# One forward transform per block in the 31-tap convolution, the second product formed across partition halves

## The chip, the core and the metric

The kernel runs on one NeuronCore of one Trainium2 chip. The metric is the device time of one execution in microseconds (us); the time before is the median of three runs. TensorE does the matmuls and the transposes, VectorE (DVE in the profile) and ScalarE (ACT) read their results out of PSUM and work on SBUF, GpSimd (POOL) does side work, SyncE (SP) issues most of the DMAs.

## The reference, cut to what matters

The model has four layers; each has a token mixer and a convolutional gated MLP, for 256 context tokens and 256 latent tokens at width 1024. Layer 1 has the Conformer convolution as its mixer:

```python
def conformer_conv(h, w1, b1, wdw, bdw, lng, lnb, w2, b2):
    a = h @ w1 + b1
    u = a[..., :D_MODEL] * jax.nn.sigmoid(a[..., D_MODEL:])
    u = dwconv(u, wdw, bdw)
    u = jax.nn.silu(layernorm(u, lng, lnb))
    return u @ w2 + b2
```

`dwconv` is a depthwise convolution with 31 taps along the tokens, one filter for each of the 1024 channels. Only this step is touched.

## The kernel before, in words

All matmuls that need full accuracy are done as three (`mm3`, lines 153 to 158): both operands are split into a high and a low part, and high times high, high times low and low times high are accumulated. `split` (lines 166 to 168) makes the two parts: ScalarE writes the high part (line 167), then VectorE subtracts it (line 168). `load_w` (lines 132 to 148) does the same to each weight load of 1 MB: two VectorE subtractions of 128x1024 at line 145.

The convolution is done in the frequency domain, with blocks of at most 128 tokens. There are 2 token streams with 3 blocks each, and 4 groups of 256 channels: 24 block units. Each passes through three steps on TensorE, each followed by work on the other engines:

- `flip_in` (line 914): two transposes of the block to tokens-on-partitions, then `split`.
- `freq` (line 926): the forward transform. The 128 output partitions hold 64 cosine rows and 64 sine rows. The transform is run twice, with the rows in the order cosine, sine (matrix 0) and in the order sine, cosine (matrix 1), 3 matmuls of 256 columns each. VectorE multiplies the first result with the filter's table `KA[hc][0]` and the second with `KA[hc][1]` (line 936), adds the two products (line 937), and the sum is split (lines 167, 168).
- `back` (line 942): the inverse transform, 3 matmuls; a VectorE instruction (`stt`, line 164) adds the bias and sums the rows, ScalarE takes the squares (line 956).

`conv` (line 980) is a generator of one channel group: it yields after each step, and takes `back` of two steps ago, then `freq` of one step ago, then `flip_in`. `run()` (line 997) lets every active generator make one step; one such call is called a round below. A step has two blocks in most rounds. The rounds lie between units of 24 matmuls of the first projection (lines 1013 to 1030): for channel tiles 2 to 5 the unit has matmuls of 512 columns, for tiles 6 and 7 of 256 columns. After each pair of units, `glu` (line 1002) writes U[o] with a sigmoid on ScalarE and an `stt` on VectorE; the next `flip_in` reads U. After the last unit follow `layer_norm(0)` (line 959), two more rounds (lines 1036 and 1038) with matmuls of the conditioning in front of them (line 222, issued by `fill`), the transposes back (`turn`, line 1040, TensorE at line 1048, ScalarE at 1052), and the second projection.

TensorE's instructions are issued in the order of the program text (a manual schedule, line 1340). The order on the other engines is chosen by the framework's scheduler, not written by hand. Waits between engines are put in by the framework. PSUM tiles come from a pool of 7 banks, working tiles in SBUF from a pool of 35.

Of the kernel before, what the change touches and what calls it, by code (L numbers as in the profile page):

```python
# [16 lines left out]
ALU = mybir.AluOpType  # L17
AX = mybir.AxisListType

P = 128  # L20
# [59 lines left out]
def kernel(ctx: ExitStack, tc: tile.TileContext, xT, cT, cB, ada0, ada2, adaT1, adaT2, adaT3, prm, rows, rope, w_c, w_ug, w_o,  # L80
# [11 lines left out]
    def ps_mm():  # L92
        return pm.tile([P, T], F32, tag="mm", name="mm")
# [59 lines left out]
    def mm3(ps, a, b, start, stop):  # L153
        ah, al = a
        bh, bl = b
        nc.tensor.matmul(out=ps, lhsT=r(ah), rhs=r(bh), start=start, stop=False)  # L156
        nc.tensor.matmul(out=ps, lhsT=r(ah), rhs=r(bl), start=False, stop=False)  # L157
        nc.tensor.matmul(out=ps, lhsT=r(al), rhs=r(bh), start=False, stop=stop)  # L158

    def both(t, f):  # L160
        return f(t[0]), f(t[1])
# [4 lines left out]
    def split(hi, lo, src):  # L166
        nc.scalar.activation(out=r(hi), in_=src, func=AF.Copy)  # L167
        nc.vector.tensor_tensor(out=r(lo), in0=src, in1=hi, op=ALU.subtract)  # L168
# [722 lines left out]
    def conformer(li, nm):  # L891
        h = (HH, HL)
        b1 = col("cf_b1")
        raw = e_tile()
        nc.sync.dma_start(out=raw[:, 0:3 * P], in_=c_dft)
        dh, dl = g_tile(), g_tile()
        split(dh[:, 0:3 * P], dl[:, 0:3 * P], raw[:, 0:3 * P])
        brow = [e_tile(), e_tile()]
        KA = [[e_tile(), e_tile()] for _ in range(2)]
        for hc in range(2):  # L900
# [25 lines left out]
        def freq(g, s, b):  # L926
            c0, c1 = CGRP[g]
            w, hc, f0 = (c1 - c0) * P, c0 // 4, (c0 % 4) * P
            n = CBLK[b][1]
            v = VT.pop((g, s, b))  # L930
            t = []
            for i in range(2):
                ps = ps_mm()
                mm3(ps[:, 0:w], both((dh, dl), lambda a: a[0:n, i * P:(i + 1) * P]), v, True, True)
                t.append(e_tile()[:, 0:w])
                nc.vector.tensor_tensor(out=t[i], in0=ps[:, 0:w], in1=KA[hc][i][:, f0:f0 + w], op=ALU.mult)
            nc.vector.tensor_tensor(out=t[0], in0=t[0], in1=t[1], op=ALU.add)
            zh, zl = duo(w)
            split(zh[:, 0:w], zl[:, 0:w], t[0])
            Z[g, s, b] = (zh[:, 0:w], zl[:, 0:w])  # L940

        def back(g, s, b):
            c0, c1 = CGRP[g]
            w, hc, f0 = (c1 - c0) * P, c0 // 4, (c0 % 4) * P
            o0, n, p0 = CBLK[b][2:5]
            ps = ps_mm()
            mm3(ps[0:nb, 0:w], both((dh, dl), lambda a: a[:, 2 * P + p0:2 * P + p0 + nb]), Z.pop((g, s, b)), True, True)
            if f0 == 0:
                Y[hc, s, b] = e_tile()
            stt(Y[hc, s, b][0:n, f0:f0 + w], ps[0:n, 0:w], 1.0, brow[hc][0:n, f0:f0 + w], ALU.mult, ALU.add,  # L950
                accum_out=ysum[0:n, 3 * s + b, g:g + 1])
            i = 3 * s + b
            if g == 0:
                nc.gpsimd.tensor_scalar(out=shift[:, i:i + 1], in0=ysum[:, i, 0:1], scalar1=-1.0 / w, scalar2=None, op0=ALU.mult)
            junk = e_tile()
            nc.scalar.activation(out=junk[0:n, 0:w], in_=Y[hc, s, b][0:n, f0:f0 + w], func=AF.Square,
                                 bias=shift[0:n, i:i + 1], accum_out=vsum[0:n, i, g:g + 1])
# [423 lines left out]
def _tables():  # L1381
# [46 lines left out]
    g = np.concatenate([2.0 / m * c, 2.0 / m * s])  # L1428
    g[0] = 1.0 / m
    g[hf] = alt / m  # L1430
    c_dft = np.concatenate([np.concatenate([c, sn]).T, np.concatenate([sn, c]).T, g], 1).astype(f32)
    kk = np.arange(CONV_W) - CPAD
    tk = 2.0 * np.pi * (np.outer(kk, np.arange(hf)) % m) / m
    ca, sa = np.cos(tk), np.sin(tk)
    cn = ca.copy()
    cn[:, 0] = 1.0 - 2.0 * (kk % 2)
    c_k = np.concatenate([ca, cn, sa, -sa], 1).astype(f32)
    return rope, ztab, decay, dft, c_dft, c_k


# [84 lines left out]
```

## Time and profile before

| | us |
|---|---|
| median of the runs before | 2188.6 |
| lowest and highest of 3 runs | 2184.32 and 2189.11 |
| span of the profiled execution, first to last instruction | 2185.3 |

For the profiled execution the span is what is listed; the median of the runs lies 3.3 us above it and the lowest run 1.0 us below it. Rows of a timeline begin with the start in us and the duration in us of one instruction, or of several merged ones (x2: two in a row), then engine, line, operation, output and inputs, and in brackets the idle time of the engine in front of it with what released it.

### The profile page before, as it was taken

How to read it: one execution, taken by the hardware profiler on the slowest of the kernel's cores; microseconds unless marked ns; L12 is line 12 of the kernel's file. 1: busy time of each engine (PE TensorE's matmuls, PEld its weight loads, DVE VectorE, ACT ScalarE, POOL GpSimd, SP SyncE). 2: the span in 40 equal slices, each digit the busy share in tenths (PEclk: the TensorE clock that was granted, in tenths of full speed). 3: DMA queues.
4: the chain of work that ended last, by engine and by line, in shares of the span. 5: the costliest groups of instructions: out<-in, count | busy, mean ns of one | idle time of the engine just before them, and what ended most of it. 6: DMA issues, size and time to landing. Idle time of an engine off the chain costs nothing. (4 is left out here: it accounts for less than half of the span.)

```text
span 2185.3 us, 32167 instructions
## 1 busy us (share of the span) xinstructions
PE 2109.3 (97%) x12058; PEld 1801.1 (82%) x12058; DVE 1554.5 (71%) x2795; ACT 1286.7 (59%) x2774; POOL 257.7 (12%) x573
## 2 busy tenths in 40 slices
PE   5899999999999999999999999999999998898999
PEld 2767888888888979888888988898888887668999
DVE  4778368889756765668775677757979856976665
ACT  3688457677634465547654443456868754875553
POOL 2375210000020001000000200020000002620000
PEclk9999999999999999999999999999999999999999
DMA  8434134545432152444443222224555531114542
GB/s 316 171 115 159 67 122 174 212 174 197 170 129 83 54 195 86 152 152 170 177 169 103 95 78 78 97 78 157 193 192 193 209 110 48 59 42 157 188 177 94
DMA packets 49048, 305.36 MB, mean 140 GB/s; under 512 B 5597, under 2 KB 7133, under 8 KB 16252
## 3 DMA queue, kind: packets, MB, share of 16 engines
q1 hardware_dynamic: 47680, 301.17, 38.9%
q10 hardware_dynamic: 1212, 2.14, 0.3%
q8 instruction: 95, 1.56, 0.3%
q14 instruction: 61, 0.50, 0.1%
HBM read 299.09 MB, written 4.19 MB: 139 GB/s over the span
## 5 line engine op out<-in xcount | busy, mean ns | idle before, releaser
L156 PE MATMUL mm<-hh,whi 128*128 128x512 f32 (+1 forms) x1856 | 657.1, 354 | 0.0
L157 PE MATMUL mm<-hl,whi 128*128 128x512 f32 (+1 forms) x1856 | 654.4, 353 | 0.0
L158 PE MATMUL mm<-hh,wlo 128*128 128x512 f32 (+1 forms) x1856 | 654.3, 353 | 0.0
L145 DVE TENSOR_TENSOR wlo<-raw,whi 128x1024 fp32r<-128x1024 f32 (+2 forms) x362 | 430.9, 1192 | 289.8 <-PE mm L157 187.2
L142 ACT ACTIVATE whi<-raw 128x1024 fp32r<-128x1024 f32 (+3 forms) x370 | 374.9, 1019 | 238.0 <-PE mm L158 157.7
L156 PEld LDWEIGHTS mm<-hh,whi 128*128 128x128 f32 x1856 | 351.2, 189 | 51.6 <-issue 5.0
L158 PEld LDWEIGHTS mm<-hh,wlo 128*128 128x128 f32 x1856 | 351.0, 189 | 47.8
L157 PEld LDWEIGHTS mm<-hl,whi 128*128 128x128 f32 x1856 | 351.3, 189 | 46.3
L264 ACT ACTIVATE e<-e 128x512 f32<-128x512 f32 x512 | 315.9, 620 | 82.0 <-DVE e L263 82.0
L156 PE MATMUL mm<-g,whi 128*128 128x512 f32 (+1 forms) x936 | 318.7, 340 | 0.0
L157 PE MATMUL mm<-g,whi 128*128 128x512 f32 (+1 forms) x936 | 317.2, 339 | 0.0
L158 PE MATMUL mm<-g,wlo 128*128 128x512 f32 (+1 forms) x936 | 317.2, 339 | 0.0
L263 DVE TENSOR_TENSOR e<-raw,e 128x512 f32<-128x512 f32 x512 | 315.2, 683 | 0.0
L316 POOL TENSOR_TENSOR e<-e 128x256 f32<-128x256 f32 (+1 forms) x69 | 66.4, 962 | 1297.0 <-ACT e L314 1296.0
L157 PEld LDWEIGHTS mm<-g,whi 128*128 128x128 f32 x936 | 178.0, 190 | 19.6
L156 PEld LDWEIGHTS mm<-g,whi 128*128 128x128 f32 x936 | 178.0, 190 | 19.5
L158 PEld LDWEIGHTS mm<-g,wlo 128*128 128x128 f32 x936 | 178.1, 190 | 19.1
L167 ACT ACTIVATE g<-e 128x512 fp32r<-128x512 f32 (+1 forms) x137 | 76.3, 558 | 139.3 <-DVE e L512 48.3
L164 DVE SCALAR_TENSOR_TENSOR e<-mm,par,e 128x510 f32<-128x510 f32 (+3 forms) x186 | 126.1, 678 | 13.8 <-ACT e L506 9.8
L164 DVE SCALAR_TENSOR_TENSOR x<-mm,mod,x 128x256 f32<-128x256 f32 x192 | 85.3, 477 | 53.1 <-PE mm L158 52.9
L168 DVE TENSOR_TENSOR g<-e,g 128x512 fp32r<-128x512 f32 (+1 forms) x137 | 81.9, 598 | 55.7 <-ACT g L167 55.3
L506 ACT ACTIVATE e<-mm,par 128x512 f32<-128x512 f32 (+1 forms) x88 | 63.1, 717 | 63.5 <-PE mm L158 58.9
(260 smaller groups left out, 2850.2 us busy)
## 6 DMA issues: line engine op xcount, KB each, us to landing
raw<-in_w_fup_dram SPq DMA_DIRECT2D x88, 1024.0 KB, 4.8
raw<-in_adaT_dram SPq DMA_DIRECT2D x64, 1024.0 KB, 4.8
raw<-in_ada_dram SPq DMA_DIRECT2D x32, 1024.0 KB, 5.0
raw<-in_w_fd_dram SPq DMA_DIRECT2D x32, 1024.0 KB, 4.8
raw<-in_w_fd_dram SPq DMA_DIRECT2D x16, 768.0 KB, 5.1
raw<-in_w_p_dram SPq DMA_DIRECT2D x12, 1024.0 KB, 4.8
raw<-in_w_hi_dram SPq DMA_DIRECT2D x12, 1024.0 KB, 4.8
raw<-in_w_o_dram SPq DMA_DIRECT2D x8, 1024.0 KB, 4.8
```

The lines of the kernel that those rows point to most:

```text
L142: nc.scalar.activation(out=r(hi[:, 0:n]), in_=part, func=AF.Copy)
L145: nc.vector.tensor_tensor(out=r(lo[:, 0:n]), in0=part, in1=hi[:, 0:n], op=ALU.subtract)
L156: nc.tensor.matmul(out=ps, lhsT=r(ah), rhs=r(bh), start=start, stop=False)
L157: nc.tensor.matmul(out=ps, lhsT=r(ah), rhs=r(bl), start=False, stop=False)
L158: nc.tensor.matmul(out=ps, lhsT=r(al), rhs=r(bh), start=False, stop=stop)
L164: nc.vector.scalar_tensor_tensor(out=o, in0=a, scalar=s, in1=b, op0=op0, op1=op1, **kw)
L167: nc.scalar.activation(out=r(hi), in_=src, func=AF.Copy)
L168: nc.vector.tensor_tensor(out=r(lo), in0=src, in1=hi, op=ALU.subtract)
L263: nc.vector.tensor_tensor(out=t, in0=raw[:, q * D + (i % 2) * T:q * D + (i % 2 + 1) * T], in1=sb[i], op=ALU.mult)
L264: nc.scalar.activation(out=t, in_=t, func=AF.Copy, accum_out=asum[:, 2 * u + q, i // 2, i % 2:i % 2 + 1])
L316: nc.gpsimd.tensor_tensor(out=self.acc[:, a:b], in0=self.acc[:, a:b], in1=t[:, a:b], op=ALU.add)
L506: nc.scalar.activation(out=t[:, c0:T], in_=pg[:, c0:T], func=AF.Identity, bias=bd[:, li, j:j + 1], scale=wd[:, li, j, 1:2])
```

## The change

`freq` transforms each block once. One PSUM tile holds cosine rows in partitions 0 to 63 and sine rows in 64 to 127. Two VectorE instructions of 64 partitions each multiply one half with the table of the sine product and write the result into the other half of the output tile; a third multiplies the whole tile with `KA[hc][0]`. The table's second half has its sign order swapped to fit, matrix 1 is left out of the constant that is loaded, and `back` finds its matrix 128 columns earlier.

```diff
-        nc.sync.dma_start(out=raw[:, 0:3 * P], in_=c_dft)
+        nc.sync.dma_start(out=raw[:, 0:2 * P], in_=c_dft)
         dh, dl = g_tile(), g_tile()
-        split(dh[:, 0:3 * P], dl[:, 0:3 * P], raw[:, 0:3 * P])
+        split(dh[:, 0:2 * P], dl[:, 0:2 * P], raw[:, 0:2 * P])
...
-            t = []
-            for i in range(2):
-                ps = ps_mm()
-                mm3(ps[:, 0:w], both((dh, dl), lambda a: a[0:n, i * P:(i + 1) * P]), v, True, True)
-                t.append(e_tile()[:, 0:w])
-                nc.vector.tensor_tensor(out=t[i], in0=ps[:, 0:w], in1=KA[hc][i][:, f0:f0 + w], op=ALU.mult)
+            ps = ps_mm()
+            mm3(ps[:, 0:w], both((dh, dl), lambda a: a[0:n, 0:P]), v, True, True)
+            t = [e_tile()[:, 0:w], e_tile()[:, 0:w]]
+            hf = P // 2
+            for at, to in ((0, hf), (hf, 0)):
+                nc.vector.tensor_tensor(out=t[1][to:to + hf], in0=ps[at:at + hf, 0:w], in1=KA[hc][1][at:at + hf, f0:f0 + w], op=ALU.mult)
+            nc.vector.tensor_tensor(out=t[0], in0=ps[:, 0:w], in1=KA[hc][0][:, f0:f0 + w], op=ALU.mult)
             nc.vector.tensor_tensor(out=t[0], in0=t[0], in1=t[1], op=ALU.add)
...
-            mm3(ps[0:nb, 0:w], both((dh, dl), lambda a: a[:, 2 * P + p0:2 * P + p0 + nb]), Z.pop((g, s, b)), True, True)
+            mm3(ps[0:nb, 0:w], both((dh, dl), lambda a: a[:, P + p0:P + p0 + nb]), Z.pop((g, s, b)), True, True)
...
-    c_dft = np.concatenate([np.concatenate([c, sn]).T, np.concatenate([sn, c]).T, g], 1).astype(f32)
+    c_dft = np.concatenate([np.concatenate([c, sn]).T, g], 1).astype(f32)
...
-    c_k = np.concatenate([ca, cn, sa, -sa], 1).astype(f32)
+    c_k = np.concatenate([ca, cn, -sa, sa], 1).astype(f32)
```

## Rows read from the trace of the kernel before

**Rows 1.** The page: span's clock, and busy time, share and instructions of each engine

```profile
core 0: 2185.3 us, clock 0.990
...
PE 2109.3 (97%) x12058; PEld 1801.1 (82%) x12058; DVE 1554.5 (71%) x2795; ACT 1286.7 (59%) x2774; POOL 257.7 (12%) x573
```

**Rows 2.** Windows: length, busy PE, PEld, DVE, ACT, POOL, clock, DMA share, GB/s

```profile
684.00:731.00 47.00, 47.00 (x264) 40.90 (x263) 31.59 (x81) 20.61 (x48) 1.27 (x6) 1.00 0.19 68
731.00:770.00 39.00, 36.44 (x303) 35.52 (x305) 28.10 (x81) 17.46 (x51) 0.00 (x0) 1.00 0.16 55
770.00:787.00 17.00, 16.10 (x94) 7.83 (x87) 13.62 (x50) 11.24 (x25) 0.00 (x0) 0.80 0.52 189
787.00:1200.00 413.00, 411.87 (x2107) 347.02 (x2107) 278.08 (x440) 233.01 (x493) 15.88 (x35) 1.00 0.42 148
```

**Rows 3.** Timeline of PE: a round's first and last `freq` matmul, then `back`

```profile
744.35 0.28 PE L156 MATMUL mm<-g 75*128 75x256 f32 x1
...
745.66 0.28 PE L158 MATMUL mm<-g 113*128 113x256 f32 x1
...
749.55 0.28 PE L157 MATMUL mm<-g 128*98 128x256 f32 x1
```

**Rows 4.** Timeline of PE: its waits between 731 and 777 us

```profile
735.60 0.58 PE L920 MATMUL tr<-ident,e 128*113 128x128 f32 x3 [0.72 <-DVE e L164]
...
755.87 0.58 PE L920 MATMUL tr<-ident,e 128*113 128x128 f32 x3 [0.77 <-DVE e L164]
...
765.39 0.36 PE L157 MATMUL mm<-g 128*98 128x256 f32 x1 [1.06 <-DVE g L168]
...
776.60 4.33 PE L1048 MATMUL tr<-ident,e 60*128 60x60 f32 x22 [0.40 <-ACT e L975]
```

**Rows 5.** Line 936, both products of every block: count, min/median/max ns

```profile
L936 DVE TENSOR_TENSOR e<-mm,e x48: 402/414/426, 684.6 to 778.3; 128x256 f32<-128x256 f32 x48
```

**Rows 6.** Timeline of DVE: the chain of one round with two blocks

```profile
744.91 0.78 DVE L936 TENSOR_TENSOR e<-mm,e 128x256 f32<-128x256 f32 x2
745.72 0.42 DVE L937 TENSOR_TENSOR e<-e 128x256 f32<-128x256 f32 x1
746.06 0.74 DVE L936 TENSOR_TENSOR e<-mm,e 128x256 f32<-128x256 f32 x2
746.73 0.41 DVE L168 TENSOR_TENSOR g<-e,g 128x256 fp32r<-128x256 f32 x1
747.06 0.41 DVE L937 TENSOR_TENSOR e<-e 128x256 f32<-128x256 f32 x1
748.02 0.42 DVE L168 TENSOR_TENSOR g<-e,g 128x256 fp32r<-128x256 f32 x1 [0.54 <-ACT g L167]
```

**Rows 7.** Timeline of DVE, attention: the second reads partitions 64 up, writes 0 up

```profile
151.50 0.67 DVE L783 TENSOR_REDUCE mx<-mm 128x2 f32<-128x512 f32 x1
152.20 0.76 DVE L164 SCALAR_TENSOR_TENSOR g<-tr,gc,g 64x512 fp32r<-64x512 f32 x1
```

**Rows 8.** Timeline of DVE: a round's last split and `glu` before 735.60

```profile
733.76 0.43 DVE L168 TENSOR_TENSOR g<-e,g 128x256 fp32r<-128x256 f32 x1 [0.54 <-ACT g L167]
...
734.80 0.75 DVE L164 SCALAR_TENSOR_TENSOR e<-mm,par,e 128x512 f32<-128x512 f32 x1
```

**Rows 9.** Timeline of DVE: what stands ahead of PE's waits at 755.87 and 765.39

```profile
753.47 0.43 DVE L168 TENSOR_TENSOR g<-e,g 128x256 fp32r<-128x256 f32 x1 [0.54 <-ACT g L167]
754.19 1.23 DVE L145 TENSOR_TENSOR wlo<-raw,whi 128x1024 fp32r<-128x1024 f32 x1 [0.29 <-PE mm L157]
...
762.77 0.41 DVE L937 TENSOR_TENSOR e<-e 128x256 f32<-128x256 f32 x1
763.77 1.23 DVE L145 TENSOR_TENSOR wlo<-raw,whi 128x1024 fp32r<-128x1024 f32 x1 [0.59 <-PE mm L157]
764.91 0.42 DVE L168 TENSOR_TENSOR g<-e,g 128x256 fp32r<-128x256 f32 x1
```

**Rows 10.** Windows (columns as in rows 2): transposes and conditioning matmuls

```profile
780.00:786.00 6.00, 6.00 (x28) 1.45 (x27) 4.55 (x13) 4.74 (x12) 0.00 (x0) 0.50 0.33 109
```

## The prediction

> **What bounds the kernel now.** I read the page first: TensorE (PE) is busy for 97% of the span, with no other engine above 82% [rows 1]. Such a share says that PE time taken away is worth looking for, but not that all of it comes back, so the next view is the windows of the stage with the convolution [rows 2]. The reader should see three different stages there. From 684 to 731 us, between units with matmuls of 512 columns, PE is busy for 47.00 of 47 us: PE alone sets the pace, and VectorE has 15 us to spare. From 731 to 770 us, between units of 256 columns, PE is busy for 36.44 of 39 us and VectorE for 28.10: PE already waits for 2.6 us. From 770 to 787 us PE does transposes and conditioning matmuls at a mean clock of 0.80. Behind that, from 787 to 1200 us, PE idles for about 1 us in 413, so a gain in the stage reaches the end. The timeline says whom PE waits for in the second stage: each wait is released by VectorE [rows 4]. Two stand at the transposes of `flip_in`, which need U from `glu`, and one at the low part that `back` needs. The fourth, at 776.60, is for the normalization's ScalarE instructions.
>
> **What the change takes from PE.** Each block loses 3 matmuls of 256 columns. Twelve such matmuls of one round start from 744.35 to 745.66 [rows 3], so one takes 1.31/11 = 0.119 us from start to start (the 0.28 us of a row is its latency). A block saves 3 x 0.119 = 0.357 us, a round with two blocks 0.71 us, the 24 blocks 8.6 us, or 0.39% of the time. That is the ceiling.
>
> **What it adds to VectorE.** A block has three products instead of two; one of 128x256 takes 414 ns [rows 5]. The half-size ones stream as many columns, so I take the same duration for them. Two products in a row take 0.74 us together, so the second starts 0.33 us after the first [rows 6]: they overlap. The trace has no product that moves between partition halves. The nearest row is the attention instruction that reads PSUM partitions 64 and up and writes partitions 0 and up: it starts at 152.20, 0.03 us after its predecessor's end at 151.50 + 0.67 = 152.17 [rows 7]. No overlap there. So the price of the third product has two ends:
> - low end: all three overlap, and a block's chain gets 0.34 us longer, a round's 0.68 us;
> - high end: each of the three starts 0.03 us behind the end of the one before, 0.44 us each. The three take 1.32 us where 0.81 pass now from the first product to the sum (744.91 to 745.72), so +0.51 us in the first block. In the second, the first product waits for the end of the sum (+0.11), and products up to the next split take 1.22 instead of 0.67 us (746.06 to 746.73), so +0.55. Together +1.17 us per round.
>
> I take the high end, because rows 7 are the nearest thing to the new instructions. The Trainium skill's page "VectorE: DVE Perf Modes", section "Two Vector instructions with no wait between them", has the same as a rule: an instruction whose inputs or output start in another quadrant of 32 partitions than those of the last instruction starts only when every earlier Vector instruction has finished. By that rule all three products are held, also the full-size one behind the two halves. It speaks against this change; without it the sum would be the low end, below.
>
> **Where the saving stays.** 12 of the 24 blocks belong to the first two channel groups, whose rounds lie in the first stage; 10 of them are followed by a full unit of 512 columns. There the chain has time: a unit of 24 such matmuls lies between it and `back`. These keep it all: 10 x 0.357 = 3.6 us.
>
> **Where the chain comes to the path.** In the second stage only 24 matmuls of 256 columns lie between `freq` and `back`. For the round shown, the first product starts at 744.91 and the second block's `back` needs its low part at 749.55 [rows 3]: 4.64 us, while the chain takes 748.44 - 744.91 = 3.53 us [rows 6]. After the change PE arrives 0.71 us sooner, 3.93 us on, and the chain takes 4.70 us (low end 4.21). PE waits for 0.77 (0.28) us that it did not wait for before. Saved 0.71, lost 0.77: the round gives nothing, -0.06 us (low end +0.43). Round by round (plus is gain):
> - The last round of the first stage: behind its chain stand, in VectorE's queue, `back`'s instruction and then `glu` (733.76, 734.80), and the transposes at 735.60 wait for that `glu` [rows 8, 4]. The end of the chain moves by 1.17 (0.68) us. From the split's end at 734.19 to `glu` at 734.80 lie 0.61 us, of which `back`'s instruction takes some 0.34 (as the spacing above); the other 0.27 swallow a part: -0.9 (-0.4).
> - Two rounds like the one shown: -0.1 (+0.9) together.
> - The round before the wait at 755.87: its chain ends at 753.90, then come a weight subtraction at 754.19, after 0.29 us of idle time, then `glu`, then the transposes [rows 9, 4]. The chain moves by 1.17 (0.68), less 0.29: -0.9 (-0.4). The idle row before it is all the cover there is.
> - The round before the wait at 765.39: two weight subtractions stand inside this chain, the second in front of the last split. The sum at 762.77 moves to about 763.9, the subtraction behind it from 763.77 to 764.3, and so does the split at 764.91 [rows 9]: -0.5 (0).
> - The next round has one block, so a chain of half the length before a unit of the same length: it keeps +0.36.
> - The last `freq` round, three blocks: PE would be done 1.07 us earlier, but the transposes behind it wait for the normalized rows, as at 776.60 [rows 4], and that chain isn't shortened: 0. The longer product chain, up to 1.7 us more, delays the high and low parts for the second projection; PE reaches that only behind the conditioning matmuls, which it runs at half clock [rows 10], and it takes the channel tiles one by one, so I count nothing for it. Without this cover it would cost up to 1.7 us.
>
> Edits counted as nothing: the constant's load and its split are a third smaller (the split goes in the queues of ScalarE and VectorE behind the norm of the first units, well before the first product at 684.6 [rows 5]; its gain is under one instruction of 0.42 us [rows 6]). One PSUM bank less is taken per block, but no wait in the stage is for a bank. The swapped table costs no instruction. No DMA is moved, and POOL isn't touched.
>
> **The sum.** 3.6 - 0.9 - 0.1 - 0.9 - 0.5 + 0.36 = 1.5 us gain at the high end; at the low end 3.6 - 0.4 + 0.9 - 0.4 + 0 + 0.36 = 4.0 us. The span of 2185.3 us [rows 1] would become 2183.8. The median of the runs lies 3.3 us above that span, and I keep the distance: 2188.6 - 1.5 = 2187.1 us. The runs before differ by 4.8 us among themselves, so about 0.2% (4.4 us) is what can be told from no change.
>
> **The rivals.**
> - Overlap after all: the half products run like the pairs at 744.91, the low end: 2188.6 - 4.0 = 2184.6 us. For it: pairs do overlap [rows 6]. Against it: rows 7.
> - All of PE's time comes back: 2188.6 - 8.6 = 2180.0 us. It needs an order on VectorE in which `glu` and the splits come ahead of what stands before them now; the order is the scheduler's, and may change. For it: VectorE's busy time after the change is about 28.1 + 9 x 0.5 = 32.6 us (nine blocks between 731 and 770) in a stage of some 36 us: it fits, just. Against it: the four waits [rows 4], three of which lie behind the very chain that gets longer.
> - Slower, by the clock. In the 6 us from 780 on PE runs at 0.50 of its clock, after some 3 us of transposes only [rows 10]. The change takes half the matmuls out of the last `freq` round, right before, and leaves waits in their place. If the lower level (1.2 GHz) began some 4 us sooner, with the transposes at 776.60, that stretch of 4.33 us [rows 4] could take up to twice as long: net 1.5 - 4.0, so 2188.6 + 2.5 = 2191.1 us. It decides from the point where the low level costs more than the 1.5 us gained: at half speed that is 3 us of PE's work sooner. For it: the row with the low clock follows a thin stretch. Against it: nine dense matmuls of that round are left, and the clock stood at full level through all waits of the second stage [rows 2].
> - The change does nothing that can be seen: VectorE takes back the 3.6 us of the first stage as well, 2188.6 us. Against it: 15 us of slack there [rows 2].
>
> **How the numbers follow.** Forecast 0.48; overlap 0.22; all of it 0.12; slower by the clock 0.10; nothing 0.08. The range leaves out most of the full gain below and little above: from 2181.0 to 2191.5 us. Faster by over 0.2% (under 2184.2) takes the full gain (0.12), half of the overlap case (0.11) and a little of the forecast (0.04): 0.27. Slower by over 0.2% (over 2193) takes the clock case with a bad draw and little else: 0.08. The rest is 0.65.
>
> **What would show it.** Right: 36 `freq` matmuls less in each half of the groups; three products per block of about 0.41 us that don't overlap; the first stage about 3.6 us shorter; more waits of PE for `glu` and for the low part between 731 and 770 us, 2 to 3 us more in all. Wrong: product pairs 0.34 us apart; no new waits, and a stage 8 us shorter; a low clock ahead of 779 us; or a different order on VectorE, with `glu` ahead of the products, which would move every one of these waits.

## The result: slower by 13 us, and the profile after

The changed kernel takes 2201.5 us (median of 4 runs, 2195.3 to 2206.4) against 2188.2 for the kernel before beside it (2184.3 to 2189.1). The ratio is 1.0064, with a 95% interval of 1.0044 to 1.0083. The forecast was 2187.1 us, and the upper end of the range was 2191.5.

The page after, first the span with its clock, then the line of the engines (compare [rows 1]):

```profile
core 0: 2201.3 us, clock 0.985
...
PE 2118.4 (96%) x11986; PEld 1800.8 (82%) x11986; DVE 1570.2 (71%) x2819; ACT 1286.6 (58%) x2774; POOL 257.3 (12%) x573
```

TensorE has the 72 matmuls less that were announced, and yet is busy for 9 us longer: it ran more of its work at the lower clock (mean 0.985, before 0.990). VectorE has 24 instructions more.

To see where the time went I cut the stage in three, by landmarks that every variant has: **A**, from the first transposes of `flip_in` to those of the seventh round that has any; **B**, from there to the first transposes of `turn`; **C**, from there to the last transposes of `turn`. Windows of the kernel before, in these three stretches (columns as in [rows 2]):

```profile
677.65:734.67 57.02, 57.02 (x326) 49.94 (x324) 36.92 (x92) 24.53 (x56) 1.27 (x6) 1.00 0.21 74
734.67:775.60 40.93, 37.93 (x309) 35.01 (x307) 30.45 (x99) 19.62 (x53) 0.00 (x0) 1.00 0.25 84
775.60:804.20 28.60, 28.14 (x186) 19.38 (x184) 17.86 (x61) 18.04 (x42) 1.47 (x2) 0.87 0.46 174
```

The same stretches of the changed kernel:

```profile
683.12:741.75 58.63, 54.69 (x289) 46.02 (x288) 45.39 (x106) 24.88 (x58) 2.19 (x6) 0.99 0.21 72
741.75:788.20 46.45, 38.85 (x273) 33.59 (x271) 35.13 (x105) 18.59 (x52) 0.00 (x0) 0.94 0.21 71
788.20:821.10 32.90, 30.91 (x185) 20.95 (x185) 21.16 (x66) 19.31 (x43) 1.45 (x2) 0.77 0.44 157
```

A is 1.6 us longer, B 5.5, C 4.3: 11.4 us in all. TensorE had no idle time in A and now has 3.9 us; in B its idle time goes from 3.0 to 7.6 us although it has fewer matmuls; and its mean clock falls from 1.00 to 0.94 in B and from 0.87 to 0.77 in C. Behind C little differs: 1381.1 us to the end before, 1380.2 after. The spans differ by more, 16.0 us, because the work ahead of the stage took 5.5 us longer in this execution (683.1 to 677.6). Of that work the kernels here change only the load and split of the constant, and its end lay anywhere from 676.9 to 684.0 us from one kernel's profile to the next. So the stage is compared from its own first transposes.

Where TensorE waits now: three waits in A, then its last and longest, then the two longest of B (timeline of PE; compare [rows 4]):

```profile
698.23 0.50 PE L156 MATMUL mm<-hh,whi 128*128 128x512 f32 x1 [0.52 <-DVE e L164]
712.29 0.36 PE L157 MATMUL mm<-g 128*98 128x256 f32 x1 [0.96 <-DVE g L168]
728.00 0.50 PE L156 MATMUL mm<-hh,whi 128*128 128x512 f32 x1 [0.50 <-DVE e L164]
...
740.76 0.52 PE L156 MATMUL mm<-g 128*98 128x256 f32 x1 [1.31 <-ACT g L167]
...
765.55 0.36 PE L156 MATMUL mm<-g 128*98 128x256 f32 x1 [1.89 <-ACT g L167]
...
776.84 0.36 PE L156 MATMUL mm<-g 128*98 128x256 f32 x1 [1.89 <-ACT g L167]
```

Before, TensorE waited for `glu` and once, for 1.06 us, for a low part (two waits in front of `freq`, at 772.80 and 773.46, took 0.17 and 0.28 us). Now it waits for the splits in front of `back` (L156 and L157 on a tile `g`): in two of A's rounds, and in nearly every round of B. The waits at 698.23 and 728.00 are at the first matmul of a unit, released by an eviction on VectorE; I read them as a PSUM bank that was not yet free. The prediction had found no wait for a bank in the kernel before, and priced none.

VectorE's chain of the first round (its timeline; L936 are the half products, L937 the full product, L938 the sum, L168 the split's subtraction; compare [rows 6]):

```profile
689.02 1.23 DVE L145 TENSOR_TENSOR wlo<-raw,whi 128x1024 fp32r<-128x1024 f32 x1 [3.55 <-PE mm L157]
690.26 0.86 DVE L936 TENSOR_TENSOR e<-mm,e 64x256 f32<-64x256 f32 x2
691.15 0.42 DVE L937 TENSOR_TENSOR e<-mm,e 128x256 f32<-128x256 f32 x1
691.61 0.43 DVE L938 TENSOR_TENSOR e<-e 128x256 f32<-128x256 f32 x1
692.06 0.86 DVE L936 TENSOR_TENSOR e<-mm,e 64x256 f32<-64x256 f32 x2
692.95 0.43 DVE L168 TENSOR_TENSOR g<-e,g 128x256 fp32r<-128x256 f32 x1
693.41 0.42 DVE L937 TENSOR_TENSOR e<-mm,e 128x256 f32<-128x256 f32 x1
693.87 0.42 DVE L938 TENSOR_TENSOR e<-e 128x256 f32<-128x256 f32 x1
694.84 0.42 DVE L168 TENSOR_TENSOR g<-e,g 128x256 fp32r<-128x256 f32 x1 [0.55 <-ACT g L167]
```

Nothing overlaps: each instruction starts 0.01 to 0.04 us behind the end of the one in front of it, the full product too; the last one waits for ScalarE's high part. The chain takes 694.84 + 0.42 - 690.26 = 5.00 us; the same round of the kernel before takes 3.50 us.

In two rounds of B a weight subtraction stands between the last product and the sum that needs it (same view):

```profile
774.44 0.42 DVE L937 TENSOR_TENSOR e<-mm,e 128x256 f32<-128x256 f32 x1
774.78 1.21 DVE L145 TENSOR_TENSOR wlo<-raw,whi 128x1024 fp32r<-128x1024 f32 x1
775.92 0.42 DVE L938 TENSOR_TENSOR e<-e 128x256 f32<-128x256 f32 x1
```

The sum starts 1.48 us behind the product, not 0.46 (691.15 to 691.61): 1.02 us in the chain, and TensorE's wait of 1.89 us at 776.84 follows.

The low clock in windows of its own (a stretch behind the wait of 1.31 us at 740.76, and one in `turn`; compare [rows 10]):

```profile
741.00:744.00 3.00, 3.00 (x13) 2.52 (x13) 1.85 (x6) 1.91 (x7) 0.00 (x0) 0.50 0.00 0
789.00:798.00 9.00, 8.72 (x35) 4.17 (x39) 7.57 (x20) 4.47 (x11) 0.00 (x0) 0.50 0.19 76
```

A granted clock of 0.50 is the lower level, 1.2 GHz. In C, the clock of 0.77 makes 2 x 0.23 x 32.9 = 15.1 us at half speed, against 2 x 0.13 x 28.6 = 7.4 before: half of the difference, 3.8 us, is lost. The same working gives B, at 0.94 for 1.00, a loss of 0.06 x 46.5 = 2.8 us, and A 0.6. So up to 7 of the 11.4 us are the lower clock, an estimate that counts each of these stretches as bound by TensorE.

### The profile page after: what moved, and what is told of

Same layout as the page of the kernel before. It is cut to its first block, busy times and chain, and to the rows that moved or that the text cites. A ratio compares the mean times of both kernels' runs of the same rounds, so it can differ in the third digit from the quotient of the medians.

```text
span 2201.3 us, 32050 instructions
## 1 busy us (share of the span) xinstructions
PE 2118.4 (96%) x11986; PEld 1800.8 (82%) x11986; DVE 1570.2 (71%) x2819; ACT 1286.6 (58%) x2774; POOL 257.3 (12%) x573
## 4 chain that ended last, share of the span: by engine, by line
PE 54%; ACT 2%; DVE 2%; POOL 1%; issue 1%; ACTq 0%; POOLq 0%; DVEq 0%
PE mm L156 16%; PE mm L157 16%; PE mm L158 16%; PE mm L442 2%; PE mm L448 1%; PE mm L832 1%; PE tr L811 0%; ACT hh L364 0%; PE mm L347 0%; DVE mx L777 0%; POOL rsy L201 0%; ACT g L794 0%; ACT g L814 0%; ACT whi L142 0%; ACT e L343 0%
## 5 line engine op out<-in xcount | busy, mean ns | idle before, releaser
L156 PE MATMUL mm<-hh,whi 128*128 128x512 f32 (+1 forms) x1856 | 658.4, 355 | 1.0 <-DVE e L164 1.0
L157 PE MATMUL mm<-hl,whi 128*128 128x512 f32 (+1 forms) x1856 | 655.7, 353 | 0.0
L145 DVE TENSOR_TENSOR wlo<-raw,whi 128x1024 fp32r<-128x1024 f32 (+2 forms) x362 | 430.5, 1192 | 290.3 <-PE mm L157 177.5
L156 PEld LDWEIGHTS mm<-hh,whi 128*128 128x128 f32 x1856 | 351.3, 189 | 52.7 <-issue 4.0
L157 PEld LDWEIGHTS mm<-hl,whi 128*128 128x128 f32 x1856 | 351.5, 189 | 46.6
L156 PE MATMUL mm<-g,whi 128*128 128x512 f32 (+1 forms) x936 | 318.2, 340 | 0.0
L157 PE MATMUL mm<-g,whi 128*128 128x512 f32 (+1 forms) x936 | 316.6, 338 | 0.0
L157 PEld LDWEIGHTS mm<-g,whi 128*128 128x128 f32 x936 | 176.8, 189 | 19.7
L156 PEld LDWEIGHTS mm<-g,whi 128*128 128x128 f32 x936 | 176.8, 189 | 19.5
L168 DVE TENSOR_TENSOR g<-e,g 128x512 fp32r<-128x512 f32 (+1 forms) x137 | 81.9, 598 | 56.6 <-ACT g L167 55.6
L164 DVE SCALAR_TENSOR_TENSOR x<-mm,mod,x 128x256 f32<-128x256 f32 x192 | 85.1, 476 | 50.8 <-PE mm L158 50.6
```

The source lines that it names most:

```text
L145: nc.vector.tensor_tensor(out=r(lo[:, 0:n]), in0=part, in1=hi[:, 0:n], op=ALU.subtract)
L164: nc.vector.scalar_tensor_tensor(out=o, in0=a, scalar=s, in1=b, op0=op0, op1=op1, **kw)
```

## The experiments

All with the stretches as above, from one profiled execution each, and the ratio to the kernel before run beside it. That kernel's median was 2188.0 us beside e1 to e4 and e13 to e16, but 2184.4 beside e5 to e8 and 2187.0 beside e9 to e12, so times of different sets are compared by their ratios. "Forward" is how often a block is transformed.

| kernel | forward | A | B | C | ratio and 95% interval |
|---|---|---|---|---|---|
| before | 2 | 57.0 | 40.9 | 28.6 | |
| the change | 1 | 58.6 | 46.5 | 32.9 | 1.0064 [1.0044, 1.0083] |
| e1, two products in place | 1 | 53.4 | 37.6 | 30.5 | 0.9968 [0.9956, 0.9979] |
| e2, third product in place | 1 | 55.8 | 42.7 | 32.9 | 1.0022 [1.0011, 1.0033] |
| e3, halves in the kernel before | 2 | 59.1 | 44.1 | 27.9 | 1.0048 [1.0031, 1.0065] |
| e4, ScalarE moves the halves | 1 | 63.5 | 57.6 | 30.7 | 1.013 [1.011, 1.015] |
| e5, change, forward transforms first | 1 | 59.6 | 53.5 | 31.2 | 1.009 [1.0072, 1.0109] |
| e6, before, forward transforms first | 2 | 57.4 | 42.7 | 28.1 | 1.0017 [1.0007, 1.0028] |
| e7, change, wide instructions | 1 | 54.3 | 41.4 | 30.7 | 1.002 [1.0008, 1.0032] |
| e8, e7 and e5 together | 1 | 56.2 | 50.8 | 31.1 | 1.0061 [1.0046, 1.0076] |
| e9, change, weights on GpSimd | 1 | 55.1 | 46.9 | 31.2 | 1.005 [1.0036, 1.0064] |
| e10, before, wide instructions | 2 | 57.0 | 40.9 | 29.8 | 1.0009 [0.9997, 1.0021] |
| e11, e7 and e9 together | 1 | 54.3 | 42.9 | 31.6 | 1.0014 [1.0004, 1.0024] |
| e12, before, weights on GpSimd | 2 | 56.7 | 41.1 | 26.8 | 1.0002 [0.999, 1.0015] |
| e13, wide change early, before late | mixed | 54.3 | 40.1 | 26.9 | 0.9978 [0.9969, 0.9988] |
| e14, change in late groups only | mixed | 57.1 | 48.2 | 30.0 | 1.0025 [1.0014, 1.0035] |
| e15, e9 and the next weights too | 1 | 54.7 | 47.5 | 31.8 | 1.0046 [1.0034, 1.0058] |
| e16, change in early groups only | mixed | 57.9 | 42.1 | 28.2 | 1.0014 [1.0005, 1.0023] |

### What the third product and the halves cost

e1 forms the second product as one full instruction in place, so that a block has two products again (the move between the halves is left out):

```diff
-            for at, to in ((0, hf), (hf, 0)):
-                nc.vector.tensor_tensor(out=t[1][to:to + hf], in0=ps[at:at + hf, 0:w], in1=KA[hc][1][at:at + hf, f0:f0 + w], op=ALU.mult)
+            nc.vector.tensor_tensor(out=t[1], in0=ps[:, 0:w], in1=KA[hc][1][:, f0:f0 + w], op=ALU.mult)
```

> One forward transform per block, but only two full-size products, both in place: the swap of the halves is left out, and with it the third VectorE instruction. PSUM tiles per round are as in the changed kernel (6, not 8). Theory (VectorE's longer chain is the whole loss): most of the 8.6 us of matmuls come back, 2179 to 2184 us, against 2188 before and 2201 after; the chain of a two-block round is 3.5 us as before, products of a block 0.33 to 0.37 us apart. Rival (PSUM tiles: with 6 per round instead of 8 a unit's bank waits for another reader): still slower than before, 2190 us or more, with PE waiting for back's instruction at the head of units.

e2 has three products again, all of 128 partitions and in place; the third goes to columns that nobody reads (the move between the halves is left out here too):

```diff
+            for o in (t[1], junk):
+                nc.vector.tensor_tensor(out=o, in0=ps[:, 0:w], in1=KA[hc][1][:, f0:f0 + w], op=ALU.mult)
```

> One forward transform, three full-size products that all read and write from partition 0 on: the table product is done twice, the second time into columns that nothing reads; the swap is left out. The same number of VectorE instructions as the changed kernel, none of them in another partition half. Theory (the loss comes from instructions in another half, each of which starts only behind the end of the one before): the three products overlap, 0.33 us apart, a round's chain is about 4.2 us, and the time is 2182 to 2190 us. Rival (only the count of instructions matters): as the changed kernel, 2197 us or more.

e3 keeps both transforms of the kernel before and cuts its second product in two half instructions that stay in their own partitions:

```diff
+                for q in ((slice(0, P),) if i == 0 else (slice(0, P // 2), slice(P // 2, P))):
+                    nc.vector.tensor_tensor(out=t[i][q], in0=ps[q, 0:w], in1=KA[hc][i][q, f0:f0 + w], op=ALU.mult)
```

> The kernel before with its two transforms; only the second product is done in two instructions of 64 partitions, each in its own half, so nothing moves between halves. PE has all its old work, VectorE three products. Theory (instructions that start in another half wait for the end of the one before): the lower half's product and the one behind it are held, a chain is 0.7 to 1.2 us longer, and since no matmul is saved the time is 2198 to 2212 us. Rival (only a write into the other half is dear): products 0.33 us apart, and 2189 to 2196 us.

e1 took 2181.4 us, e2 2192.0, e3 2197.3 beside 2188.0 for the kernel before. The windows of e1, stretches A and B:

```profile
677.89:731.25 53.36, 52.86 (x290) 45.52 (x288) 37.46 (x94) 25.19 (x58) 1.27 (x6) 1.00 0.23 79
731.25:768.90 37.65, 34.63 (x274) 30.92 (x272) 29.12 (x96) 18.56 (x51) 0.00 (x0) 1.00 0.25 87
```

So the transform's time does come back where VectorE's part stays as it was: A falls by 3.7 us, and TensorE is hardly idle there. e1 has the change's six PSUM tiles per round, so these aren't the loss. e2 and e3 fell outside what their theories gave (2182 to 2190 and 2198 to 2212 us). The chain of a round is 3.51 us in e1, 4.30 in e2, 5.00 in the change. A chain longer by 0.79 us costs 10.6 us of median, another 0.70 us costs 9.5; in the stage alone (A, B and C together) it is 9.9 and 6.6. These are two prices, the instruction itself and its hold (that it starts only at the end of the one in front), of the same order. e2 is also the prediction's low end, where the third product overlaps: 2184.6 us were given for it, 2192.0 came. e2's chain shows the overlap that the change lacks (timeline of DVE):

```profile
691.30 0.75 DVE L936 TENSOR_TENSOR e<-mm,e 128x256 f32<-128x256 f32 x2
691.96 0.42 DVE L168 TENSOR_TENSOR g<-e,g 128x256 fp32r<-128x256 f32 x1
692.29 0.42 DVE L937 TENSOR_TENSOR e<-mm,e 128x256 f32<-128x256 f32 x1
```

Here an instruction starts 0.33 us behind the start of its predecessor, in the change 0.43 to 0.46. This agrees with the rule of the Trainium skill, page "VectorE: DVE Perf Modes", section "Two Vector instructions with no wait between them", that an instruction whose inputs or output begin in another quadrant than the last one's waits for all earlier ones to finish. e3 shows that moving between halves isn't needed for it (timeline of DVE; L937 are the products, the x2 a full one and the half at partitions 0 to 63, the last the half at 64 to 127):

```profile
687.14 0.75 DVE L937 TENSOR_TENSOR e<-mm,e 128x256 f32<-128x256 f32 x2
687.82 0.41 DVE L168 TENSOR_TENSOR g<-e,g 128x256 fp32r<-128x256 f32 x1
688.26 0.43 DVE L937 TENSOR_TENSOR e<-mm,e 64x256 f32<-64x256 f32 x1
688.72 0.43 DVE L938 TENSOR_TENSOR e<-e 128x256 f32<-128x256 f32 x1
```

The half at partition 0 overlaps like a full product; the half at partition 64, which stays in its own partitions, waits for the end of the split in front of it, and starts 0.44 us behind it. One more instruction per block with such a hold costs the kernel before 9 us of median.

e4 has ScalarE copy the halves crosswise, and VectorE form two products:

```diff
-                nc.vector.tensor_tensor(out=t[1][to:to + hf], in0=ps[at:at + hf, 0:w], in1=KA[hc][1][at:at + hf, f0:f0 + w], op=ALU.mult)
+                nc.scalar.activation(out=sw[to:to + hf], in_=ps[at:at + hf, 0:w], func=AF.Copy)
+            nc.vector.tensor_tensor(out=t[1], in0=sw, in1=KA[hc][1][:, f0:f0 + w], op=ALU.mult)
```

> One forward transform; ScalarE copies the two halves of the result crosswise into SBUF (two instructions of 64x256 per block, some 0.37 to 0.42 us each, 48 in all), VectorE does the two full-size products of the kernel before. The result is the reference's. Theory: VectorE has its old load, ScalarE (busy for half of the stage) takes 18 us more beside; a chain gets about 0.5 us longer by the copies: 2180 to 2190 us, at or below before. Rival (any step more in the chain costs as much, on whichever engine): 2196 us or more.

2215.7 us, the slowest of all. The chain, now from ScalarE's first copy, takes 5.56 us, and the second block's copies stand behind the first block's split in ScalarE's queue. Taking work from VectorE doesn't help if the path from `freq` to `back` gets longer by it.

### Where the reader of the chain stands

e5 changes the order in a round, the same for e6 from the kernel before:

```diff
-                for f, at in ((back, i - 2), (freq, i - 1), (flip_in, i)):
+                for f, at in ((freq, i - 1), (back, i - 2), (flip_in, i)):
```

> The changed kernel, but in each round the two forward transforms are issued ahead of the two back transforms of the round before, instead of behind them. VectorE's chain (first product to last subtraction, 5.00 us for two blocks) stays as it is; what waits for it on TensorE comes later by the six matmuls of two forward transforms (0.21 us each, so 1.3 us). Theory (the lost time is TensorE waiting for the end of that chain, and the low clock behind these waits): TensorE's idle time in the stage falls from 13.5 to about 5 us, the stage from 138 to 122 to 127 us, total 2185 to 2191. Rival 1 (VectorE's time itself is what limits, wherever the reader stands): stage 135 us or more, total 2198 to 2203. Rival 2 (the forward transforms, now 1.3 us earlier behind the transposes, wait for the split of these instead): TensorE's waits move to VectorE's and ScalarE's split of the transposes, total above 2195.

> The same move of the forward transforms ahead of the back transforms in the kernel before. Theory: its chain of 3.50 us is nearly covered, TensorE is idle for only 3.45 us of the stage, so at most these can be had: 2184.5 to 2188.5. Rival 2 of the run above (the split of the transposes is late instead): above 2190, and the waits name that split. Against the run above it tells what the move does where there are no halves.

My theory failed here: 2204.8 us for e5 where it wanted 2185 to 2191, and 2190.3 for e6, with the kernel before at 2184.4. The waits of TensorE in e5's stage (us in total, times, longest):

```profile
PE mm L156 <- ACT g L167: 8.4, 5, 3.4
PE tr L920 <- DVE e L164: 3.8, 3, 1.3
PE mm L156 <- DVE e L937: 2.9, 2, 1.5
```

In the changed kernel the first stood at 6.8 us, all but 0.2 of it in front of `back`, and the other two weren't there. In e5 only 1.5 of its 8.4 us are in front of `back`; the rest is in front of `freq`. The transposes now wait for `glu`, the next unit's first matmul for a bank that a product has to free, and the forward transform for the split of the transposes, which stands behind the chain in the queues of VectorE and ScalarE: rival 2. A reader that comes later gains nothing where all others stand behind the same queue. So it isn't the chain's length alone that counts, but what is queued on VectorE in a round.

e7 makes the queue shorter: the two blocks of a round lie side by side in one PSUM tile, and the products, the sum and the split are done once on 512 columns. e8 has e5's order on top of it. e10 is the same widening for the kernel before. In the cut, `wide` and `spectrum` are views of the tile and of the table over both blocks:

```diff
+            for j, (s, b) in enumerate(todo):
+                mm3(ps[:, j * w:(j + 1) * w], both((dh, dl), lambda a: a[0:n, 0:P]), VT.pop((g, s, b)), True, True)
+            for at, to in ((0, hf), (hf, 0)):
+                nc.vector.tensor_tensor(out=wide(t[1])[to:to + hf], in0=wide(ps)[at:at + hf], in1=spectrum(1, at), op=ALU.mult)
+            nc.vector.tensor_tensor(out=wide(t[0]), in0=wide(ps), in1=spectrum(0, 0), op=ALU.mult)
```

> The changed kernel, with the two blocks of a round side by side in one PSUM tile, so that the two half products, the full product, the sum and the split each run once on 512 columns and not twice on 256: 5 VectorE instructions and one of ScalarE per round for 10 and 2. Estimate from the rows of 256 columns (0.42 us, of which some 0.15 us would be saved by each pair): chain of about 4.5 us, but it can begin only when both transforms are done, 0.6 us later, and the two blocks no longer overlap, ScalarE's part standing bare. Theory (length of the chain from the end of the transforms): about as the change or a little better, 2195 to 2202. Rival (the number of held VectorE instructions): with half as many, 2186 to 2192.

> Both edits: wide instructions, and the forward transforms ahead of the back transforms. Theory: 1.3 us of slack more per round covers most of what is left of the chain: 2181 to 2187, below both kernels. Rival 1 (VectorE's time itself): as the wide kernel without the move, 2 us either way. Rival 2 (late split of the transposes): above the wide kernel without the move.

> The kernel before with both transforms kept, and the two blocks of a round side by side in one PSUM tile per transform: two products, a sum and a split of 512 columns in place of twice as many of 256. Against the changed kernel in the same wide form (2188.8 in the runs before) it tells what the one transform itself brings where VectorE has room. Theory (full queue of VectorE): 8 instructions of a round become 4, some 0.6 us less; the kernel before has little idle time left (2.6 us in the first part), so 2182 to 2187. Rival (chain alone: the blocks no longer overlap and begin 0.7 us later): 2187 to 2193.

e7 takes 2188.8 us, 0.2% above the 2184.4 beside it: the number of held instructions (the rival) came true, the length of the chain alone didn't. Its chain of a round (timeline of DVE; L943 the half products, L944 the full one, L945 the sum):

```profile
685.78 1.39 DVE L943 TENSOR_TENSOR e<-mm,e 64x512 f32<-64x512 f32 x2
687.20 0.69 DVE L944 TENSOR_TENSOR e<-mm,e 128x512 f32<-128x512 f32 x1
687.93 0.69 DVE L945 TENSOR_TENSOR e<-e 128x512 f32<-128x512 f32 x1
689.38 0.69 DVE L168 TENSOR_TENSOR g<-e,g 128x512 fp32r<-128x512 f32 x1 [0.76 <-ACT g L167]
```

4.29 us in place of 5.00, with 5 instructions for 10. A falls to 54.3 us, nearly e1's 53.4; B, at 41.4, does no better than the kernel before. e8 loses as e5 did (2199.3 us, 2181 to 2187 expected). e10 (2187.8 us) is the kernel before within the uncertainty: TensorE had no idle time in A to win back.

### What else stands in VectorE's queue

In the changed kernel the weight subtraction (L145, 1.22 us) has no idle time in front of it in four of its eight places in A; before, it always had some, 1.37 us or more. A round there lasts 7.34 us on TensorE (e1), and VectorE has to do 5.0 us of chain, 1.22 of subtraction, 0.74 of split, 0.8 of two evictions and `glu`'s 0.75 in every second round. That is over 8 us in such a round, and the trace has the same: the chains of the change start at 690.26, 698.55 and 706.32 us, 8.29 and 7.77 us apart. e9 gives the subtraction of outputs 2 to 7 to GpSimd, e12 does so in the kernel before, e11 in e7:

```diff
+        lo_eng[0] = nc.gpsimd
         for o in range(2, 6):
             w = load(o)
...
-            nc.vector.tensor_tensor(out=r(lo[:, 0:n]), in0=part, in1=hi[:, 0:n], op=ALU.subtract)
+            (lo_eng[0] or nc.vector).tensor_tensor(out=r(lo[:, 0:n]), in0=part, in1=hi[:, 0:n], op=ALU.subtract)
```

> The changed kernel, with the subtraction of the weights' second parts (1.22 us on VectorE, one per round of the first ten rounds or so) given to GpSimd for the weights of outputs 2 to 7 of this stage. The chain itself stays: three products of 0.45 us per block. Theory (what counts is all that stands in VectorE's queue of a round: chain, split of the transposes, evictions and the weight subtraction, against a round of some 7.2 us on TensorE; the change filled it): VectorE has 12 subtractions of 1.22 us less, its queue fits again, TensorE's idle time in the first part of the stage falls from 10.7 to 3 to 5 us, the low clock there goes, total 2188 to 2193 against 2201. Rival (only the length of the chain between the forward and the back transform counts; the subtraction stands outside it in most rounds): not below 2197. Rival 2 (GpSimd takes about twice as long, about 2.5 us from 1.28 us for 512 columns, and the weights are late, or it slows VectorE's instructions beside it): VectorE's instructions lengthen, or TensorE waits for GpSimd; 2200 or more.

> The kernel before with the weight subtraction of this stage on GpSimd. Theory: its VectorE had room (63 of 94 us busy in the first part), TensorE is idle there for 2.6 us, so it gains at most these: 2183 to 2188. It is the control of the changed kernel with the same edit: if this one gains as much, the edit says nothing of the change.

> The changed kernel with wide instructions and with the weight subtraction on GpSimd. Theory (full queue): of the wide kernel's 6.8 us of idle TensorE in the first part 4 to 5 go, total 2182 to 2186, below both kernels. Rival (chain alone): 2187 to 2190, as the wide kernel.

e9 is at 2198.7 us, so in the total the rival came nearer. By stretches both were right, each in one place: A falls from 58.6 to 55.1 us, and its first five intervals from transposes to transposes are 6.63, 7.34, 13.48, 6.65 and 7.35 us, e1's within 0.01 (the change: 6.64, 7.34, 15.50, 6.95, 7.34). The sixth, the last of A, stays at 13.66, with 14.86 in the change and 11.90 in e1. B stays at 46.9. The control e12 gains 0.3 us in A and nothing in B. e11 (2190.5 us, 2182 to 2186 expected) adds nothing to e7, whose rounds already fitted.

### Early and late rounds apart

e16 makes the change for channel groups 0 and 1 only, whose rounds lie behind long units, e14 for groups 2 and 3 only (`g >= 2` in the same line); e15 is e9 with the end of its stretch moved behind the next projection's loads, and so puts the next projection's weight subtractions, those inside the chain, on GpSimd as well. The edit of e16:

```diff
-                for f, at in ((back, i - 2), (freq, i - 1), (flip_in, i)):
+                for f, at in ((back, i - 2), ((freq_once if g < 2 else freq), i - 1), (flip_in, i)):
```

> From the kernel before: only groups 0 and 1 as in the change (one transform, half products of 256 columns), groups 2 and 3 with two transforms. Theory (in the changed kernel the first six rounds lose only where a weight subtraction and the chain fill VectorE's round): first six rounds 57 to 58.6 us, the rest 36 us, total 0 to 2 us above before. With the run of the late groups it splits the change's 13 us.

> From the kernel before: only groups 2 and 3 as in the change. Theory: the first six rounds 57.0 us as before; from there to the last transposes about 41 us for 36 (chain of 5 us behind units of 2.8 us), and some 4 us more at the low clock after it; total 7 to 11 us above before. Rival (the loss is spread over all rounds alike): 4 to 6 us above before, and the groups 0 and 1 alone as much.

> The changed kernel with all weight subtractions of the stage on GpSimd, those of the next step's weights too, which stand between the last product and the sum in two of the short rounds. Theory (what stands inside the chain pays in full): the first six rounds 54 to 55 us (58.6; 55.1 with the first loads alone), the two rounds of 13.3 us fall to 11.5 to 12, the rest to 38 to 40 us (42.0), total 2190 to 2195. Rival (only the chain's own instructions count): the rest stays at 41 to 42 us, total 2197 or more.

e16 is 0.14% slower (2190.3 us), e14 0.25% (2193.5). Their stages are 1.6 and 8.7 us longer than that of the kernel before, 10.3 of the change's 11.4; the medians add up to less, 2.2 and 5.5 of 13 us, and the rest isn't assigned. e14's median lies in the range of its rival (4 to 6 us), but e16's isn't as much, as that rival would have it. By the stages, then, most of the loss is in the late rounds, where 24 matmuls of 0.12 us lie between `freq` and `back`. Part of it is the clock: e14's B has a mean of 0.89, which by the working above is 5.3 of its 48.2 us. The two long waits are there in e14 with the same length (timeline of PE):

```profile
757.06 0.36 PE L156 MATMUL mm<-g 128*98 128x256 f32 x1 [1.89 <-ACT g L167]
...
769.71 0.53 PE L156 MATMUL mm<-g 128*98 128x256 f32 x1 [1.89 <-ACT g L167]
```

e15 should have shortened them, and made them 2.46 us. The sum took the subtraction's place as the slow one. VectorE in that round:

```profile
757.10 0.42 DVE L939 TENSOR_TENSOR e<-mm,e 128x256 f32<-128x256 f32 x1
757.56 2.00 DVE L940 TENSOR_TENSOR e<-e 128x256 f32<-128x256 f32 x1
760.05 0.42 DVE L170 TENSOR_TENSOR g<-e,g 128x256 fp32r<-128x256 f32 x1
```

and GpSimd at that time:

```profile
756.78 2.50 POOL L147 TENSOR_TENSOR wlo<-raw,whi 128x1024 fp32r<-128x1024 f32 x1 [26.11 <-PE mm L160]
```

The sum reads two tiles in SBUF and ends 0.28 us after GpSimd does (759.56 to 759.28); the product at 757.10, which reads one tile in PSUM, is not slowed. So what the subtraction in the chain costs is read from the rows, 1.02 us in each of two rounds, and not shown by taking it away. But the wait grew by 0.57 us (2.46 for 1.89) where the sum's 1.58 us took the place of those 1.02, in both rounds: what is added to this chain, TensorE waits for in full.

### The version that beats both

e13 takes the one transform, in wide form, for groups 0 and 1 (e7's `freq`, here `freq_once`, with the tables of the kernel before), and leaves groups 2 and 3 as they were:

```diff
                     if 0 <= at < n:
+                        if f is freq and g < 2:
+                            freq_once(g, *todo[at])
+                            continue
```

> From the kernel before: groups 0 and 1, whose transforms run between units of 512 columns, take one transform in wide form with two half products; groups 2 and 3, between units of 256 columns, keep two transforms. Theory (between long units TensorE is the bound and the transform's time is kept; between short ones the chain on VectorE is the bound and decides): from the first transposes to those six rounds later 54.3 to 55 us (57.0 before, 58.6 in the changed kernel), from there to the last transposes 36 us as before, total 2 to 3 us below before: 2184 to 2187. Rival (no gain is kept anywhere, since each round's chain grows): the first six rounds take 57 us or more, total 2188 or more.

2182.7 us against 2188.0: the ratio is 0.9978, and its interval lies below 1. Its windows, A, B and C:

```profile
683.97:738.25 54.28, 52.86 (x290) 45.55 (x289) 40.62 (x75) 23.28 (x50) 1.27 (x6) 1.00 0.22 78
738.25:778.30 40.05, 37.77 (x309) 35.05 (x308) 29.90 (x98) 19.51 (x53) 0.00 (x0) 1.00 0.24 86
778.30:805.20 26.90, 26.46 (x186) 19.01 (x184) 17.71 (x60) 17.87 (x41) 1.47 (x2) 0.94 0.47 182
```

A is 2.7 us shorter than before, as expected, and the total lies just below the 2184 to 2187 us given; B is 0.9 shorter. The 1.7 us in C come from less time at the low clock (0.94 for 0.87), in a stretch that the edit doesn't touch; e12, with both transforms, has it too (26.8 us). I count 3 to 4 us as e13's own.

## Why the prediction was wrong

- **What the change takes from TensorE: right.** 3.6 us were forecast for the ten blocks of the first stage; in e1 the five intervals with these blocks are 3.9 us shorter, and A, with two blocks more, 3.7.
- **What it adds to VectorE: the right end, mis-sized.** The high end, "each of the three starts 0.03 us behind the end of the one before", is what the trace shows, but a round's chain got longer by 1.50 us, not 1.17. The prediction left two holds in the second block out: the first block's split comes between its half products and its full one, and the full product behind it (692.95 to 693.41) and the sum behind that (693.41 to 693.87) each start 0.46 us on, where 0.33 passed before. The low end, 0.68, is e2's 0.79.
- **"There the chain has time ... These keep it all": the first step that failed.** A should have gained 3.6 - 0.9 = 2.7 us (the 0.9 is for a wait that before stands just behind A's end) and lost 1.6. By intervals, four of the first five did keep all or most of their saving (6.64, 7.34, 6.95 and 7.34 us for 7.35, 8.20, 7.37 and 8.22), but the third went from 14.23 to 15.50, and the sixth, from which the 0.9 was taken, from 11.65 to 14.86. The 15 us of slack in 47 were a mean over the stage. What counts is each round: some 8 us of queue on VectorE in a round of 7.34, and the intervals suggest that what is left over is passed on to the next. e9 takes the subtraction out, and the first five come back to e1's; the sixth doesn't.
- **"Where the chain comes to the path": the second, and the dearer.** The terms for B come to -0.1 - 0.9 - 0.5 + 0.36 = -1.1 us; it was -5.5. A shorter chain would not have saved the account: e2's is near the low end, which gave 4.0 us of gain, and e2 lost 4. Each round was charged with what the chain exceeds its slack by, from TensorE's waits of before. But with the longer chain the scheduler's order put a weight subtraction inside it in two rounds (763.50 and 774.78), where the prediction allowed for 0.5 us in one; the waits moved from `glu` to the split itself; and at the lower clock (2.8 us in B by the estimate above) the matmuls behind a wait took longer still. e14 has this loss without the early groups.
- **Nothing for what lies behind the last round: the third.** C was counted at 0 and lost 4.3 us, 3.8 of it by the clock. The rival "slower, by the clock" had the place and the size (4 us), but as an alternative with a chance of 0.10. It came on top of the rest, and a low clock stood ahead of 779 us too, the prediction's own sign of being wrong (741 to 744). It needs no long chain: e1 also has a clock of 0.81 in C, with only the matmuls gone. How it depends on the work ahead of it was not taken apart; kernels with two transforms have 26.8 to 29.8 us there, those with one throughout 30.5 to 32.9.
- **The other rivals.** "Overlap after all" did not come: the products hold each other, and e2 shows that overlap would not have been enough. "All of PE's time comes back" needed another order on VectorE; e1 reaches 2181.4 us, near its 2180.0, but by leaving the third product out. "VectorE takes back the 3.6 us of the first stage" was near the truth for A, which lost 1.6 us more than that, and got 0.08.
- **The chance of 0.08 for slower** rested on pricing each stretch by its mean slack and on treating as rivals what can happen together. (The terms of the sum add up to 1.56 and 4.06 us, put down as 1.5 and 4.0; that is no part of the error.)

## What to carry to other kernels

Slack on an engine that works in order is counted per round of the loop, with all that stands in its queue there: evictions, splits, weight preparation. A transform on TensorE that looks redundant can be the cheaper side of a trade, if what replaces it lengthens the chain between two of TensorE's own steps; taking it out paid where long units cover the chain (and there with wide instructions, e13, not with the change's, e16), and not where units are short, so the same change can be made in one part of a loop and left out in the other. And fewer, wider vector instructions won back about two thirds of the change's loss (a ratio of 1.0020 for 1.0064).

## What the runs showed of the hardware

- Instructions of 64 partitions cost as much as those of 128 (422 to 414 ns). In the change they hold their neighbours: 0.43 to 0.46 us from start to start, against 0.33 for full ones. In e3, where nothing crosses partitions, the half at partition 64 is held (0.44 us) and the half at partition 0 isn't.
- A VectorE sum of two SBUF tiles beside a GpSimd instruction took 2.00 us, not 0.42, ending 0.28 us after it; in e9 and e15 other sums took 0.95 to 0.97 us, in e12 0.71 to 1.48. The Trainium skill's page "SBUF — State Buffer", section "Who interferes with whom", says that such an instruction contends with one of GpSimd that reads SBUF, and that the later one waits; the trace agrees. e9's expectation allowed for it; e15's did not allow for a cost (1.58 us) above that of the subtraction of 1.22 us that it replaced.
- In the changed kernel a stretch at 1.2 GHz (741 to 744 us) follows two waits of 0.48 and 1.31 us within 2 us, between units where the kernel before, with single waits of up to 1.06 us, stayed at 2.4 GHz throughout. The wait alone doesn't decide it: behind the wait of 1.89 us at 765.55 the clock stayed at 1.00, behind the equal one at 776.84 it fell (0.59 from 778 to 780 us).
